# The high parts of q's, k's, gate's and value's weights begin 64 bytes further on in their tiles

## The chip, the cores and the metric

The kernel runs on one core of one Trainium2 chip. The metric is the device time of one execution in microseconds. Three runs of the kernel before took 966.67, 966.77 and 966.89 us; the median is 966.77 us.

## The reference

One layer of a bidirectional encoder for 256 tokens of width 2048, in float32:

```
h = rmsnorm(x, norm1_g);  q, k, v, u = split(h @ w_in)        # 1536, 512, 512, 512 columns
a = rmsnorm(window_attention(q, k, v, sink), attn_out_g)      # 12 heads of 128, 4 of k and v
f = rmsnorm(fourier_mix(u, w_fourier), fourier_out_g)         # 4 groups of 128
x = x + concat(a, f) @ w_out
h = rmsnorm(x, norm2_g);  gate, val = split(h @ w_up)         # 5504 columns each
x = x + (gelu(conv3(gate) + dw_b) * val) @ w_down
y = rmsnorm(x, normf_g)
```

The weights are 2048 x 2560 (`w_in`), 2048 x 2048 (`w_out`), 2048 x 11008 (`w_up`) and 5504 x 2048 (`w_down`). The work is matrix products.

## The kernel before

**Two parts for each operand.** Products run in the type float32r. To keep precision, each operand is split into a high part (a copy in float32r) and a low part (the operand less its high part). A product is then the sum of three: high by high, high by low, low by high.

**Units.** Weights come in units, tiles of 128 partitions x 2048 elements. `load` (L139) starts the DMA of a unit into one of three `raw` buffers, on SyncE's queue. `split` (L153) makes the high part on ScalarE (L160) and the low part on VectorE (L161); both go to tiles that `parts_of` (L145) takes, three buffers for `hi` and three for `lo`. The tiles are 2176 elements wide, 128 more than a unit has. `parts_of` returns 2048 of them, from element `s` on. For units 0 to 7 (u's four and v's four) `s` is `UV_SHIFT`, 16 elements or 64 bytes; for all others it is 0. The units in order: 0 to 3 u, 4 to 7 v, 8 to 23 q and k (16 heads), 24 to 39 the output projection, and then 86 of gate and value, 43 each, with the late rows of the down projection among them.

**Two ways to multiply.** `moving_weights` (L290) streams the weights, 512 columns at a time, past a part of the activations that is loaded into TensorE; three matmuls for each block of 128 rows (L296 to L298). It serves u, v, the output projection and the late rows of the down projection; `by_parts` (L1022 to L1024) and `last_product` (L1161 to L1163) do the same with other operands. `still_weights` (L302) loads a 128 x 128 block of the weights and streams the activations past it. It serves q, k, gate and value. The activations lie in the four tiles `hT` (after the second norm they are named hU), where each block of 128 rows has its 256 high and 256 low columns side by side. So one matmul over 512 columns does high by high and high by low (L307), and one over 256 columns low by high (L308):

```python
for k in kk:
    h = hT[k // 4][:, k % 4, :]
    s = slice(k * P, (k + 1) * P)
    nc.tensor.matmul(ps, hi[:, s], h, start=k == 0, stop=False)
    nc.tensor.matmul(ps[:, 0:S], lo[:, s], h[:, 0:S], start=False, stop=k == NK - 1)
```

A unit has 16 such pairs of matmuls. Each matmul has a load of its weights of its own, which the profile shows as PEld.

**Order.** The program is written out by hand; there is no scheduler. `unit` (L339) runs a unit's matmuls, then posts of earlier units, then the split of the unit two ahead; that split starts the load of the unit three further on. In the feed-forward part a list (`ff_items`, L68) gives the order: gate and value tiles of the first eight, then, for four groups, gate and value units that take turns with products of the down projection (`split_product` L908, seven products of two column halves, 56 in all), and at the end the late rows, the last three tiles' gate and value, and the last products. `ff_step` (L949) does there what `unit` does. The products' weights are split into the same `hi` and `lo` buffers, from element 0 on.

Of the kernel before, what the change touches and what calls it, by code (L numbers as in the profile page):

```python
# [30 lines left out]

U_HEAD, U_ROW = 16, 768

UV_SHIFT = 16

V_G2, V_GA, V_GF, V_DW, V_DB, V_SINK = 0, 16, 28, 32, 161, 204
V_N = 216
# [30 lines left out]
def ff_items():  # L68


    def ups(tiles):
        return [(kind, j) for j in tiles for kind in ("gate", "val")]

    items = ups(range(8))
    for g in range(N_GROUPS):
        todo = {
            "u": ups(range(8 * g + 8, 8 * g + 16)),
            "s": [("product", g, c, p) for c in range(2) for p in PRODUCTS[c]],
        }
        items += [todo[c].pop(0) for c in PATTERN]  # L80
        assert not any(todo.values())
    items += [("down", 0, c) for c in range(4)] + ups(LAST)
    items += [("down", 1, c) for c in range(4)] + [("last", c) for c in range(4)]
    return items
# [3 lines left out]
def block_kernel(  # L88
# [26 lines left out]
    def f32(ap):  # L115
        return ap.bitcast(F32)
# [4 lines left out]

    units = [(w_u_x[i], 2048) for i in range(4)] + [(w_in[i], 2048) for i in range(20)]
    units += [(w_out[i], 2048) for i in range(16)]
    n_front = len(units)
    items, up_index = ff_items(), {}
    for n, it in enumerate(items):
        if it[0] == "product":
            continue
        up_index[n] = len(units)
        if it[0] in ("gate", "val"):  # L130
            units.append((w_up[2 * it[1] + (it[0] == "val")], 2048))
        elif it[0] == "down":
            units.append((w_down_late[4 * it[1] + it[2]], 2048))
        else:
            units.append((w_down_last[it[1]], 512 * len(LAST)))
    RAW = 3
    raws, halves = {}, {}

    def load(i):  # L139
        if i < len(units) and i not in raws:  # L140
            src, n = units[i]
            raws[i] = wp.tile([P, 2048], F32, tag="raw", name=f"raw{i}", bufs=RAW)
            nc.sync.dma_start(raws[i][:, 0:n], src)

    def parts_of(i):  # L145
        s = UV_SHIFT if i < 8 else 0
        halves[i] = tuple(
            wp.tile([P, 2176], F32R, tag=h, name=f"{h}{i}", bufs=3)[:, s : s + 2048]
            for h in ("hi", "lo")
        )  # L150
        return halves[i]

    def split(i):  # L153

        if i >= len(units):
            return
        n = units[i][1]
        raw = raws[i]
        hi, lo = parts_of(i)
        nc.scalar.activation(hi[:, 0:n], raw[:, 0:n], AF.Copy)  # L160
        nc.vector.tensor_tensor(lo[:, 0:n], raw[:, 0:n], f32(hi[:, 0:n]), ALU.subtract)  # L161
        load(i + RAW)
        load_more(i + RAW)

# [29 lines left out]
    def u_part(k, o, n, m=1):  # L194

        rows = ux[k // 4][:, (k < 4) * U_HEAD :].rearrange("p (k c) -> p k c", k=4)
        return rows[:, k % 4 : k % 4 + m, o : o + n]
# [26 lines left out]
    def load_more(i):  # L224

        if i == 6:
            nc.sync.dma_start(chan, c_chan)
            nc.sync.dma_start(wfs, wf)
            nc.sync.dma_start(pos, c_pos)
        if i == 7:  # L230
            nc.sync.dma_start(vec[:, 0:V_N], vecs)
            nc.sync.dma_start(rel, c_rel)
# [118 lines left out]
    for k in range(NK):  # L351
        c, q = k // 4, k % 4
        if q == 0:
            hi, lo = (t.rearrange("p (k c) -> p k c", k=4) for t in parts_of(c))
        n = 1 if c < 2 else 2
        if k == 0:
            nc.vector.tensor_copy(hi[:, 0, :], u_part(0, 0, FW)[:, 0, :])
        split_scaled(hk(k), u_part(k, FW, S)[:, 0, :], g1[:, k : k + 1])
        if q % n == 0:
            w, h = u_part(k, 0, FW, n), hi[:, q : q + n, :]  # L360
            if k > 0:
                nc.scalar.activation(h, w, AF.Copy)
            nc.vector.tensor_tensor(lo[:, q : q + n, :], w, f32(h), ALU.subtract)
        if k < 4:

            for p, w in enumerate([hi, hi, lo]):
                for b in range(2):
                    o = p % 2 * S + b * P
                    nc.tensor.matmul(
                        ps_u[b], hk(k)[:, o : o + P], w[:, q, :],  # L370
                        start=k == 0 and p == 0, stop=False,
                    )
        else:
            for b in range(2):
                moving_weights(
                    *halves[c], 512, [k], hk, b, ps_u[b], False, k == NK - 1, q0=q
                )
        if q == 3:
            del halves[c]
# [387 lines left out]
    for n, (c, kq) in enumerate(OUT_ORDER):  # L767
        i = N_OUT + n
# [334 lines left out]
    for n, it in enumerate(items):  # L1103
# [26 lines left out]
        else:  # L1130
            kind, g, c = it
            hi, lo = halves.pop(up_index[n])
# [11 lines left out]
    i = up_index[n]  # L1144
# [147 lines left out]
```

## Time and profile before

| | |
|---|---|
| median of three runs | 966.77 us |
| profiled execution | 966.83 us |
| its span, first to last instruction | 965.1 us |
| mean granted TensorE clock | 0.998 |
| matmuls, weight loads | 5083, 5083 |
| L160, L161 (the splits) | 133 each; mean 1903 and 2276 ns |
| L307 for gate and for value | 688 each |
| L308 for gate and for value | 688 each |
| L307 for q and for k | 192 and 64 |
| DMA | 211.58 MB, 219 GB/s on the mean |

The profile is of one execution. PE is TensorE's matmuls, PEld its loads of weights, DVE VectorE, ACT ScalarE, POOL GpSimd. A row of the timeline gives the start and the duration of an instruction in microseconds, the engine, the line, what is written and read, and the shape. The duration of a matmul (0.39 us for 512 columns) holds its way through the array, and matmuls overlap; how fast they follow each other is seen from the starts. A row of the windows view gives a stretch, its length, and for each engine the busy time in it with the number of instructions in brackets.

### The profile page before, as it was taken

The numbers are of one execution on the slowest core, as the hardware profiler recorded it, in microseconds if no ns is written. First come the engines' busy times: TensorE is split into PE (matmuls) and PEld (weight loads), VectorE is DVE, ScalarE is ACT, GpSimd is POOL, SyncE is SP. The second block draws the span as 40 slices with busy tenths as digits, with TensorE's granted clock in tenths as the row PEclk, the third lists the DMA queues.
The fourth block names the chain that finished last, engine by engine and source line by source line (L and its number), as shares of the span: only waits on it lengthen the run. The fifth ranks groups of instructions, "written<-read, shape, count | busy, mean of one in ns | idle before, by whom it ended". The sixth has DMA issues, their size and how long they took to land.

```text
span 965.1 us, 12764 instructions
## 1 busy us (share of the span) xinstructions
PE 955.5 (99%) x5083; PEld 820.0 (85%) x5083; DVE 746.4 (77%) x926; ACT 535.7 (56%) x650; POOL 44.6 (5%) x59
## 2 busy tenths in 40 slices
PE   9999999999999999999999999999999999999996
PEld 7888898888888888888888888888888888888885
DVE  7658877666576679786898877988778979888675
ACT  7656766554454446555555555565555655553533
POOL 0000000000000000000000000000000000000003
PEclk9999999999999999999999999999999999999999
DMA  9844444446446675977777787776977686765532
GB/s 369 333 169 144 162 139 167 138 169 218 176 174 230 243 224 181 279 242 257 223 256 235 235 292 242 254 240 208 292 245 245 205 282 209 233 233 211 195 132 88
DMA packets 31676, 211.58 MB, mean 219 GB/s; under 512 B 3456, under 2 KB 3712, under 8 KB 7424
## 3 DMA queue, kind: packets, MB, share of 16 engines
q1 hardware_dynamic: 28016, 184.55, 51.4%
q0 software_dynamic: 3600, 26.22, 14.5%
q8 instruction: 40, 0.66, 0.3%
q14 instruction: 20, 0.16, 0.0%
HBM read 208.65 MB, written 2.10 MB: 218 GB/s over the span
## 4 chain that ended last, share of the span: by engine, by line
PE 96%; DMA 1%; DVE 1%; ACT 1%; issue 0%; SPq 0%; POOL 0%; ACTq 0%; POOLq 0%
PE ps_val L307 17%; PE ps_gate L307 17%; PE ps_val L308 8%; PE ps_gate L308 8%; PE ps_q L307 5%; PE ps_P L1022 3%; PE ps_P L1024 3%; PE ps_P L1023 3%; PE ps_q L308 2%; PE ps_a L298 2%; PE ps_a L296 2%; PE ps_a L297 2%; PE ps_N L1022 2%; PE ps_N L1024 2%; PE ps_N L1023 2%; PE ps_k L307 2%
## 5 line engine op out<-in xcount | busy, mean ns | idle before, releaser
L161 DVE TENSOR_TENSOR lo<-raw,hi 128x2048 fp32r<-128x2048 f32 (+1 forms) x133 | 302.8, 2276 | 54.8 <-ACT hi L160 54.8
L160 ACT ACTIVATE hi<-raw 128x2048 fp32r<-128x2048 f32 (+1 forms) x133 | 253.1, 1903 | 60.6 <-PE ps_l L297 25.1
L307 PE MATMUL ps_gate<-hU,hi 128*128 128x512 f32 x688 | 242.9, 394 | 0.0
L307 PE MATMUL ps_val<-hU,hi 128*128 128x512 f32 x688 | 242.8, 394 | 0.0
L308 PE MATMUL ps_val<-hU,lo 128*128 128x256 f32 x688 | 193.0, 281 | 0.0
L308 PE MATMUL ps_gate<-hU,lo 128*128 128x256 f32 x688 | 193.0, 281 | 0.0
L307 PEld LDWEIGHTS ps_gate<-hU,hi 128*128 128x128 f32 x688 | 129.4, 188 | 30.0
L307 PEld LDWEIGHTS ps_val<-hU,hi 128*128 128x128 f32 x688 | 129.3, 188 | 30.0
L308 PEld LDWEIGHTS ps_gate<-hU,lo 128*128 128x128 f32 x688 | 129.0, 187 | 1.1
L308 PEld LDWEIGHTS ps_val<-hU,lo 128*128 128x128 f32 x688 | 128.9, 187 | 1.1
L809 ACT ACTIVATE ft_g<-ps_gate 128x256 f32<-128x256 f32 x43 | 16.5, 384 | 127.5 <-PE ps_gate L308 127.5
L809 ACT ACTIVATE ft_v<-ps_val 128x256 f32<-128x256 f32 x43 | 16.5, 385 | 97.1 <-PE ps_val L308 97.0
L307 PE MATMUL ps_q<-hT,hi 128*128 128x512 f32 x192 | 68.5, 397 | 0.0
L308 PE MATMUL ps_q<-hT,lo 128*128 128x256 f32 x192 | 54.0, 281 | 0.0
L1022 PE MATMUL ps_P<-hi_P,op_P 128*128 128x512 f32 x128 | 50.2, 392 | 0.0
L1024 PE MATMUL ps_P<-lo_P,op_P 128*128 128x512 f32 x128 | 50.1, 391 | 0.0
L1023 PE MATMUL ps_P<-hi_P,op_P 128*128 128x512 f32 x128 | 49.7, 389 | 0.0
L919 DVE TENSOR_TENSOR lo_N<-sumw,hi_N 128x2048 fp32r<-128x2048 f32 x16 | 36.6, 2290 | 10.1 <-ACT hi_N L918 10.1
L307 PEld LDWEIGHTS ps_q<-hT,hi 128*128 128x128 f32 x192 | 36.1, 188 | 8.0
L811 DVE TENSOR_TENSOR fa_g<-ps_gate,ft_g 128x256 f32<-128x256 f32 x43 | 18.2, 423 | 29.3 <-ACT ft_g L809 29.3
L296 PE MATMUL ps_a<-hi,cat 128*128 128x512 f32 x96 | 37.8, 394 | 0.0
L1022 PE MATMUL ps_N<-hi_N,op_N 128*128 128x512 f32 x96 | 37.7, 393 | 0.0
(326 smaller groups left out, 1606.1 us busy)
## 6 DMA issues: line engine op xcount, KB each, us to landing
raw<-in_w_up SPq DMA_DIRECT2D x86, 1024.0 KB, 5.0
raw<-in_w_in SPq DMA_DIRECT2D x20, 1024.0 KB, 4.8
raw<-in_w_out SPq DMA_DIRECT2D x16, 1024.0 KB, 4.8
sumw<-in_w_down POOLq DMA_DIRECT2D x16, 1024.0 KB, 8.6
raw<-in_w_down_late SPq DMA_DIRECT2D x8, 1024.0 KB, 4.8
ux<-in_w_u_x SPq DMA_DIRECT2D x2, 1536.0 KB, 12.9
raw<-in_w_down_last SPq DMA_DIRECT2D x4, 768.0 KB, 4.2
xs<-in_x SPq DMA_DIRECT2D x4, 512.0 KB, 18.4
```

Source lines behind the costliest of these rows:

```text
L160: nc.scalar.activation(hi[:, 0:n], raw[:, 0:n], AF.Copy)
L161: nc.vector.tensor_tensor(lo[:, 0:n], raw[:, 0:n], f32(hi[:, 0:n]), ALU.subtract)
L296: nc.tensor.matmul(ps, ah, wh, start=first and q == q0, stop=False)
L297: nc.tensor.matmul(ps, al, wh, start=False, stop=False)
L298: nc.tensor.matmul(ps, ah, wl, start=False, stop=last and q == q0 + len(kk) - 1)
L307: nc.tensor.matmul(ps, hi[:, s], h, start=k == 0, stop=False)
L308: nc.tensor.matmul(ps[:, 0:S], lo[:, s], h[:, 0:S], start=False, stop=k == NK - 1)
L809: nc.scalar.activation(tmp, ps[:, S : 2 * S], AF.Copy)
L919: nc.vector.tensor_tensor(lo, src, f32(hi), ALU.subtract)
L1022: nc.tensor.matmul(ps, o[:, 0, p, :], hi[:, s], start=first and p == 0, stop=False)
L1023: nc.tensor.matmul(ps, o[:, 1, p, :], hi[:, s], start=False, stop=False)
L1024: nc.tensor.matmul(ps, o[:, 0, p, :], lo[:, s], start=False, stop=last and p == 3)
```

## The change

A list gives each unit two starts, one for its high and one for its low part. For u and v both stay at 16 elements. For q, k, gate and value the high part begins at 16 and the low part at 0. The output projection and the down projection stay at 0.

```diff
-UV_SHIFT = 16
+SHIFT = 16
...
     units += [(w_out[i], 2048) for i in range(16)]
+    shifts = [(SHIFT, SHIFT)] * 8 + [(SHIFT, 0)] * 16 + [(0, 0)] * 16
...
         if it[0] in ("gate", "val"):
             units.append((w_up[2 * it[1] + (it[0] == "val")], 2048))
+            shifts.append((SHIFT, 0))
+            continue
         elif it[0] == "down":
             units.append((w_down_late[4 * it[1] + it[2]], 2048))
         else:
             units.append((w_down_last[it[1]], 512 * len(LAST)))
+        shifts.append((0, 0))
...
     def parts_of(i):
-        s = UV_SHIFT if i < 8 else 0
         halves[i] = tuple(
             wp.tile([P, 2176], F32R, tag=h, name=f"{h}{i}", bufs=3)[:, s : s + 2048]
-            for h in ("hi", "lo")
+            for h, s in zip(("hi", "lo"), shifts[i])
         )
         return halves[i]
```

## The prediction

> **What bounds the kernel now.** I read the page's busy line and its chain first, then the view of who waits for whom on TensorE, and then, because that engine turns out to be full, start times of single matmuls in the timeline.
>
> ```profile
> span 965.1 us, 12764 instructions
> PE 955.5 (99%) x5083; PEld 820.0 (85%) x5083; DVE 746.4 (77%) x926; ACT 535.7 (56%) x650; POOL 44.6 (5%) x59
> ...
> PE 96%; DMA 1%; DVE 1%; ACT 1%; issue 0%; SPq 0%; POOL 0%; ACTq 0%; POOLq 0%
> ```
>
> ```profile
> PE ps_warm L243 <- POOL ones L235: 1.0, 1, 1.0
> PE ps_u L298 <- DVE lo L363: 0.5, 1, 0.5
> PE ps_l L296 <- DVE xs L1029: 0.2, 1, 0.2
> PE ps_u L369 <- ACT hT L250: 0.2, 1, 0.2
> ```
>
> TensorE (PE) is busy for 99% of the span and is 96% of the chain that ended last. All its waits for other engines sum to 1.9 us. So only one thing can move the end by more than a couple of microseconds: how far apart matmuls start. The split of the weights (L160, L161), the loads and the posts lie beside it.
>
> Most of that time is L307 and L308, `still_weights`: 16 times per unit, a matmul that streams 512 columns of h past the high part of the weights and one that streams 256 columns past the low part. I call these two a pair. 102 units (16 of q and k, 86 of gate and value) make 1632 pairs. While one matmul streams, the next one's weights are loaded (PEld): the low part's load lies beside the 512-column stream, the next high part's beside the 256-column one.
>
> How long does a pair take? The windows view on L307, with counts, and two timeline rows for q:
>
> ```profile
> core 0: us, PE busy (x) PEld busy (x), PEclk, DMA share, GB/s
> 283.98:368.78 84.80, 84.80 (x241) 44.98 (x240) 1.00 0.64 223
> 885.54:919.03 33.49, 33.49 (x96) 17.87 (x95) 1.00 0.52 187
> ```
>
> ```profile
> 158.44 0.39 PE L307 MATMUL ps_q<-hT,hi 128*128 128x512 f32 x1
> ...
> 164.08 0.40 PE L673 MATMUL ps_o<-pt,v_hi 128*128 128x256 f32 x2
> ```
>
> The first stretch runs from the first matmul of one gate unit to the end of another, with 15 units in it and no product between: 240 pairs (240 weight loads; one matmul of the 241 began before it) in 84.80 us, 353.3 ns each. The second is the last six units: 96 pairs in 33.49 us, 348.9 ns each. The q unit: 16 pairs in 5.64 us, 352.5 ns. The instructions, the addresses modulo 128 and the clock (PEclk 1.00) are the same, and still there are two rates, a slow one and a fast one. Start times show the slow one to be a cycle of three pairs:
>
> ```profile
> 295.29 0.40 PE L307 MATMUL ps_gate<-hU,hi 128*128 128x512 f32 x1
> 295.52 0.28 PE L308 MATMUL ps_gate<-hU,lo 128*128 128x256 f32 x1
> 295.64 0.39 PE L307 MATMUL ps_gate<-hU,hi 128*128 128x512 f32 x1
> 295.87 0.28 PE L308 MATMUL ps_gate<-hU,lo 128*128 128x256 f32 x1
> 295.99 0.40 PE L307 MATMUL ps_gate<-hU,hi 128*128 128x512 f32 x1
> 296.22 0.28 PE L308 MATMUL ps_gate<-hU,lo 128*128 128x256 f32 x1
> 296.35 0.40 PE L307 MATMUL ps_gate<-hU,hi 128*128 128x512 f32 x1
> ```
>
> Three pairs take 1.06 us (295.29 to 296.35). What would be the least? Streams of equal matmuls show it:
>
> ```profile
> 921.76:955.08 33.32, 33.32 (x148) 1.00 0.23 82
> ```
>
> ```profile
> 955.20 0.28 PE L1162 MATMUL ps_e<-hi,act 128*128 128x256 f32 x1
> ...
> 957.12 0.28 PE L1163 MATMUL ps_e<-lo,act 128*128 128x256 f32 x1
> ```
>
> The first stretch holds 147 matmuls of 512 columns (the 148th is the tail of an earlier one): 226.7 ns each. The second has 17 matmuls of 256 columns from the first row to the last, so 16 steps in 1.92 us, 120.0 ns each. A pair at these two is 346.7 ns, which I call the floor. The kernel pays 2.2 ns over it per pair in the fast cycle and 6.6 ns in the slow one. Rows that are rounded to 10 ns don't tell which of the two steps pays: in the cycle above the three long steps sum to 0.69 us (0.68 at the floor), the three short ones to 0.37 (0.36).
>
> **What the change does, part by part.** It moves no instruction: on all five engines the order and the waits are the same, and so are the allocations. The `hi` slice of the 102 units starts 64 bytes later. In the built program's allocation hT and hU lie at 96 modulo 128 bytes, every `hi` and `lo` tile at 32, and the operands of products, output projection and last tiles at 32. So in the two streams at the floor, and in v's (both parts already shifted to 96, hT at 96), what streams and what is loaded beside it have the same place modulo 128. In the pairs they are 64 apart, both for the high and the low part. After the change the high part's load has the same place as the h that streams; the low part's is still 64 apart.
>
> *Splits.* L160 writes, and L161 reads, a `hi` that begins 64 bytes on. v's units have that already; rows of DVE for one of them and for the first k unit, then of ACT for the same two:
>
> ```profile
> 44.02 2.29 DVE L161 TENSOR_TENSOR lo<-raw,hi 128x2048 fp32r<-128x2048 f32 x1
> 51.57 2.29 DVE L161 TENSOR_TENSOR lo<-raw,hi 128x2048 fp32r<-128x2048 f32 x1 [2.52 <-ACT hi L160]
> ```
>
> ```profile
> 38.84 1.91 ACT L160 ACTIVATE hi<-raw 128x2048 fp32r<-128x2048 f32 x1
> 49.63 1.91 ACT L160 ACTIVATE hi<-raw 128x2048 fp32r<-128x2048 f32 x1
> ```
>
> 2.29 and 2.29, 1.91 and 1.91 us: no cost. If there were one, TensorE would cover it, with DVE at 77% and ACT at 56%. The DMAs write `raw`, which stays.
>
> *Pairs.* The trace of before has no pair with the high part in the same place, so I bound it. One end is the floor, 346.7 ns, reached wherever places are the same. The other is the slow cycle, 353.3 ns, the worst that lasts. One load of the two comes to the favourable place, so I take half of what the fast cycle still pays: (346.7 + 348.9) / 2 = 347.8 ns for all pairs. The sum:
> - gate and value, slow: the 240 pairs above and, at the same rate, the 32 ahead of them: 272 x (353.3 - 347.8) = 1.5 us
> - the other 1104 pairs of gate and value: 1104 x (348.9 - 347.8) = 1.2 us
> - q and k: 256 pairs; all fast would give 0.3 us, all at 352.5 ns 1.2 us; I take 0.9 us
>
> Together 3.6 us.
>
> *Products.* They come between ups, one after each, with unshifted weights. A stretch of 13 ups and 13 products:
>
> ```profile
> 371.54:479.88 108.34, 73.23 (x209) 39.10 (x208) 1.00 0.77 239
> ```
>
> 208 pairs at 348.9 are 72.6 us, 156 product matmuls at 226.7 are 35.4 us; 0.4 us are left, 0.03 us for each change from pairs to products and back, 1.7 us for all 56. I count none of it as gained: the load beside the last 256 columns is then the product's operand, whose place stays. If pairs ran at the floor and so led into products without loss, it would be gained too.
>
> *Sum.* The profiled execution took 966.83 us, 1.73 us of it outside the span of 965.1; the median of the runs shown is 966.77, so they agree. 966.83 - 3.6 = 963.2 us.
>
> [...] The two floor streams show no sign of where a tile lies by itself: v's matmuls (33.20 to 33.65 for two) at 96 and the last tiles' at 32 both step by 0.23.
>
> ```profile
> 33.20 0.39 PE L297 MATMUL ps_v<-hi,hT 128*128 128x512 f32 x1
> ...
> 33.65 0.39 PE L296 MATMUL ps_v<-hi,hT 128*128 128x512 f32 x1
> ```
>
> [...]
>
> **The rivals.**
>
> *All the way to the floor* (part of my case, its far end): 272 x 6.6 + 1104 x 2.2 = 4.2 us, q and k 256 x up to 5.8 = 1.5, products 1.7: 7.4 us, 959.4 us. For it: every stream with the same places is at the floor. Against: the low part's load stays 64 apart, and it lies beside the long step, which seems to pay as much as the short one.
>
> *No effect.* Where the two reads do not meet at all, only the order and the mixture of 512 and 256 columns make the excess, and the place changes nothing: 966.8 us. For it: two rates exist with the same places, so something besides the place decides, and one of the two loads isn't moved. Against: nothing but the pairs is off the floor for long. [...] If the cycles are merely redrawn and all pairs fall into the fast one, it is 272 x 4.4 = 1.2 and about 0.7 for q and k: 964.9 us.
>
> *The slow cycle everywhere, slower than before.* The pairs lock into a three-pair cycle whose rate depends on how they are entered: the long gate and value stretch is slow from its entry until the first product at 368.78, and everything after is fast. A high part that moves by 64 bytes may shut the fast cycle off, because its load now asks for the same place as the 256-column stream, the shortest one, with the least time to hide a delay of the load. Its price is 353.3 - 348.9 = 4.4 ns on the 1104 pairs and about 64 of q and k that are fast: 5.1 us, 972.0 us. It decides from the point where three pairs after a product take 1.06 us and not 1.05. For it: the slow cycle is stable for 240 pairs once entered. Against: same places never show such a cycle.
>
> **How the numbers follow.** The pairs gain, between the fast cycle and the floor (959.4 to 964.9): 0.47, and the likeliest, at 963.2. No effect: 0.20, at 966.8. Slow cycle in most or all units: 0.33, up to 972.0. A measurement here tells about 0.2% from no change, 1.9 us, so the cases give faster 0.47, same 0.20, slower 0.33. The range takes the floor and the slow cycle with half a microsecond each for the stalls at q and k: 959.0 to 972.5. For my own case alone it is 959.4 to 964.9.
>
> **What the profile after would show.** My case: after the change the stretch from the second gate unit to the first product, 240 pairs, takes 83.2 to 83.7 us in place of 84.80, and the last 96 pairs about 33.4 or less in place of 33.49; splits stay at 1.91 and 2.29. No effect: both stretches as they are. Slow cycle: the last 96 pairs take 33.9 us, and an up with its product grows by 0.07 us. I am wrong in the mechanism if the pairs' rate changes while that of the three-pair cycle doesn't, if the streams of equal matmuls leave 226.7 ns, or if TensorE begins to wait for DVE or ACT.

## The result, and the profile after

The kernel after takes 965.63 us (median of 21 runs, 965.23 to 966.01); the kernel before, beside it, 966.94 us (21 runs, 966.44 to 967.70). The ratio is 0.9985, with a 95% interval of 0.9979 to 0.9991: 1.3 us or 0.15% faster, less than the 0.2% that the prediction set as its bound for a difference. The forecast was 963.2.

The page of the kernel after, its busy line and the shares of the chain that ended last:

```profile
span 963.6 us, 12764 instructions
...
PE 954.2 (99%) x5083; PEld 819.5 (85%) x5083; DVE 746.2 (77%) x926; ACT 535.7 (56%) x650; POOL 44.5 (5%) x59
...
PE 96%; DMA 1%; DVE 1%; ACT 1%; issue 0%; SPq 0%; POOL 0%; ACTq 0%; POOLq 0%
```

And all that TensorE waits for in it (in total, times, longest, us):

```profile
PE ps_warm L247 <- POOL ones L239: 1.0, 1, 1.0
PE ps_u L373 <- ACT hT L254: 0.2, 1, 0.2
PE ps_u L302 <- DVE lo L367: 0.2, 1, 0.2
PE ps_l L300 <- DVE xs L1033: 0.2, 1, 0.2
```

The number of instructions and the full TensorE are as in before, and the waits too, but for one that is 0.3 us shorter and lies ahead of the first k pair (lines of the file have moved on by four: L307 and L308 are L311 and L312 now). So the 1.3 us lie in how closely matmuls follow each other. The same three stretches of L311 as in the prediction, in the windows view of the kernel after:

```profile
283.04:367.04 84.00, 84.00 (x241) 45.01 (x240) 1.00 0.66 226
369.77:478.11 108.34, 73.42 (x209) 39.11 (x208) 1.00 0.76 239
883.94:917.54 33.60, 33.60 (x96) 17.86 (x95) 1.00 0.53 186
```

The 240 pairs ahead of the first product took 84.80 us and take 84.00: from 353.3 to 350.0 ns a pair. The last 96 took 33.49 and take 33.60: from 348.9 to 350.0, a little slower. The 13 ups with 13 products take 108.34 as before. There is one rate for gate and value now, where there were two. Its cycle in the timeline of the kernel after:

```profile
294.24 0.39 PE L311 MATMUL ps_gate<-hU,hi 128*128 128x512 f32 x1
294.48 0.27 PE L312 MATMUL ps_gate<-hU,lo 128*128 128x256 f32 x1
294.59 0.40 PE L311 MATMUL ps_gate<-hU,hi 128*128 128x512 f32 x1
294.82 0.28 PE L312 MATMUL ps_gate<-hU,lo 128*128 128x256 f32 x1
294.94 0.39 PE L311 MATMUL ps_gate<-hU,hi 128*128 128x512 f32 x1
```

Two pairs take 0.70 us (294.24 to 294.94), and then the pattern repeats. In before it was three pairs in 1.06 us.

Where the time went can be read from the starts of four matmuls. The first pair of k and the first pair of gate, in the timeline of the kernel after and then of the kernel before:

```profile
55.27 0.48 PE L311 MATMUL ps_k<-hT,hi 128*128 128x512 f32 x1
...
259.32 0.40 PE L311 MATMUL ps_gate<-hU,hi 128*128 128x512 f32 x1
```

```profile
55.41 0.48 PE L307 MATMUL ps_k<-hT,hi 128*128 128x512 f32 x1
...
260.14 0.40 PE L307 MATMUL ps_gate<-hU,hi 128*128 128x512 f32 x1
```

With the ends of the windows above, and those of the same windows of before in the prediction, this gives three stretches:

| stretch | before, us | after, us | gained, us |
|---|---|---|---|
| first k pair to first gate pair (q, k, attention, output projection) | 204.73 | 204.05 | 0.68 |
| first gate pair to first product | 108.64 | 107.72 | 0.92 |
| first product to the last six units | 516.76 | 516.90 | -0.14 |
| the last six units | 33.49 | 33.60 | -0.11 |

Together 1.35 us. The span is 1.5 us shorter because this execution also came to its first k pair 0.14 us earlier; that part of the program is not touched, and the medians differ by 1.31.

### The profile page after: what moved, and what is told of

It reads as the page before. It is cut to its first block, busy times and chain, and to the rows that moved or that the text cites. A ratio compares the mean times of both kernels' runs of the same rounds, so it can differ in the third digit from the quotient of the medians.

```text
span 963.6 us, 12764 instructions
## 1 busy us (share of the span) xinstructions
PE 954.2 (99%) x5083; PEld 819.5 (85%) x5083; DVE 746.2 (77%) x926; ACT 535.7 (56%) x650; POOL 44.5 (5%) x59
## 4 chain that ended last, share of the span: by engine, by line
PE 96%; DMA 1%; DVE 1%; ACT 1%; issue 0%; SPq 0%; POOL 0%; ACTq 0%; POOLq 0%
PE ps_gate L311 17%; PE ps_val L311 17%; PE ps_val L312 8%; PE ps_gate L312 8%; PE ps_q L311 5%; PE ps_P L1027 3%; PE ps_P L1028 3%; PE ps_P L1026 3%; PE ps_q L312 2%; PE ps_a L302 2%; PE ps_a L300 2%; PE ps_a L301 2%; PE ps_N L1027 2%; PE ps_N L1028 2%; PE ps_N L1026 2%; PE ps_k L311 2%
## 5 line engine op out<-in xcount | busy, mean ns | idle before, releaser
L311 PE MATMUL ps_val<-hU,hi 128*128 128x512 f32 x688 | 242.9, 396 | 0.0
L311 PE MATMUL ps_gate<-hU,hi 128*128 128x512 f32 x688 | 242.9, 396 | 0.0
L312 PE MATMUL ps_gate<-hU,lo 128*128 128x256 f32 x688 | 192.4, 280 | 0.0
L312 PE MATMUL ps_val<-hU,lo 128*128 128x256 f32 x688 | 192.4, 280 | 0.0
L311 PEld LDWEIGHTS ps_val<-hU,hi 128*128 128x128 f32 x688 | 129.4, 188 | 30.4
L311 PEld LDWEIGHTS ps_gate<-hU,hi 128*128 128x128 f32 x688 | 129.4, 188 | 30.4
L312 PEld LDWEIGHTS ps_gate<-hU,lo 128*128 128x128 f32 x688 | 130.0, 189 | 1.1
L312 PEld LDWEIGHTS ps_val<-hU,lo 128*128 128x128 f32 x688 | 130.0, 189 | 1.0
L311 PE MATMUL ps_q<-hT,hi 128*128 128x512 f32 x192 | 68.1, 398 | 0.0
L312 PE MATMUL ps_q<-hT,lo 128*128 128x256 f32 x192 | 53.6, 279 | 0.0
L311 PEld LDWEIGHTS ps_q<-hT,hi 128*128 128x128 f32 x192 | 36.1, 188 | 8.0
```

## The experiments

To compare kernels I write the place of a loaded block against the start of the activations that stream past it, in bytes, high part first. The places are those of the built program's allocation; the profile does not show them. The activations begin at 96 modulo 128 bytes and also modulo 256. Before is (-64, -64), after is (0, -64). "First rate" is that of the 240 pairs ahead of the first product, "last rate" that of the last 96 pairs.

The place theory was at first that each load's place by itself acts on the rate of the pairs, and in the end that the places of the two loads, taken together, do. Its rivals: that the distance between the high and the low part decides, one load's place against the other's (the distance theory, later called the step theory); that any move of a part out of a common place changes something, in the split or elsewhere, whatever the activations' place; and that what runs ahead of a pair picks its rate (the entry theory), at first with the place of no account. Each expectation tells what these give for its kernel. The kernels of a group ran on one chip beside runs of before.

| kernel | places | us | ratio to before, 95% interval | first rate, ns | last rate, ns |
|---|---|---|---|---|---|
| before | (-64, -64) | 966.9 to 967.1 | | 353.3 | 348.9 |
| after | (0, -64) | 965.63 | 0.9985 (0.9979 to 0.9991) | 350.0 | 350.0 |
| lo64 | (-64, 0) | 953.14 | 0.9856 (0.9840 to 0.9872) | 340.0 | 340.2 |
| both64 | (0, 0) | 964.50 | 0.9971 (0.9960 to 0.9982) | 346.7 | 346.7 |
| hi128 | (+64, -64) | 970.53 | 1.0034 (1.0021 to 1.0048) | 353.4 | 353.1 |
| h64 | mixed | 970.77 | 1.0036 (1.0023 to 1.0049) | 349.7 | 350.0 |
| hi256 | (+192, -64) | 967.24 | 1.0002 (0.9992 to 1.0011) | 353.3 | 349.0 |
| hi64_lo128 | (0, +64) | 963.19 | 0.9958 (0.9944 to 0.9973) | 346.7 | 346.9 |
| lo128 | (-64, +64) | 961.68 | 0.9943 (0.9928 to 0.9958) | 346.7 | 346.6 |
| h448 | (0, 0) | 969.20 | 1.0022 (1.0013 to 1.0032) | 346.7 | 353.2 |
| qk_only | q, k (0, -64) | 966.23 | 0.9992 (0.9983 to 1.0001) | 353.3 | 349.0 |
| prod64 | (-64, -64) | 970.85 | 1.0041 (1.0026 to 1.0055) | 353.3 | 349.0 |
| lo64_w64 | (-64, 0) | 954.40 | 0.9870 (0.9856 to 0.9885) | 340.0 | 350.0 |
| lo64_w192 | (-64, 0) | 967.17 | 1.0003 (0.9993 to 1.0012) | 340.0 | 340.1 |

### Which of the two parts

**lo64** moves the low parts and leaves the high ones.

```diff
-    shifts = [(SHIFT, SHIFT)] * 8 + [(SHIFT, 0)] * 16 + [(0, 0)] * 16
+    shifts = [(SHIFT, SHIFT)] * 8 + [(0, SHIFT)] * 16 + [(0, 0)] * 16
...
-            shifts.append((SHIFT, 0))
+            shifts.append((0, SHIFT))
```

> Only the low parts of q, k, gate and value begin 64 bytes on (high parts at 0). Place theory (a pair's rate is set by where each loaded block lies against the h that streams beside it, modulo 128 bytes, each load by itself): one of the two loads is in the same place as h, as in the changed kernel, but the one beside the 512-column stream; a third rate between 346.7 and 353.3 ns, not a cycle of three pairs at 353.3. Distance theory (what counts is that high and low part are 64 bytes apart from each other, so that successive loads alternate): the same as the changed kernel, 350.0 ns a pair in gate and value, 965.6 us. Entry theory (the address is irrelevant, each program redraws the cycle that it falls into): any of 346.7, 348.9, 350.0 and 353.3, with units of one kind of entry at several rates.

Measured: 953.14 us. The first and the last stretch of pairs in the windows view of lo64, and its pairs in the timeline:

```profile
281.86:363.46 81.60, 81.60 (x241) 45.00 (x240) 1.00 0.67 232
872.75:905.41 32.66, 32.66 (x96) 17.86 (x95) 1.00 0.55 192
```

```profile
294.10 0.39 PE L311 MATMUL ps_gate<-hU,hi 128*128 128x512 f32 x1
294.33 0.28 PE L312 MATMUL ps_gate<-hU,lo 128*128 128x256 f32 x1
294.44 0.39 PE L311 MATMUL ps_gate<-hU,hi 128*128 128x512 f32 x1
294.67 0.28 PE L312 MATMUL ps_gate<-hU,lo 128*128 128x256 f32 x1
294.78 0.39 PE L311 MATMUL ps_gate<-hU,hi 128*128 128x512 f32 x1
```

240 pairs in 81.60 us are 340.0 ns each, and every pair takes the same 0.34 us: no cycle over several pairs. This is below the 346.7 ns that the prediction called the floor, and none of the three theories had it. So the two parts are not alike: the low one's load, which lies beside the 512-column stream, is the one to move. The high one's load, beside the 256-column stream, does better 64 bytes off, as the next kernel shows (346.7 ns with it level, against 340.0).

**both64** moves both parts, so that all places are equal.

```diff
-            shifts.append((SHIFT, 0))
+            shifts.append((SHIFT, SHIFT))
```

(The same is done in the list for q and k.)

> High and low parts of q, k, gate and value both begin 64 bytes on, so all loads are in the same place as h modulo 128. Place theory: the floor, 346.7 ns for every pair, and products entered without loss; about 959.5 to 961 us. Distance theory: both parts have one place again, so it behaves as the kernel before: 353.3 and 348.9 ns, 966.9 us. Entry theory: no forecast, between 959 and 972 us.

Measured: 964.50 us. The first and the last stretch in its windows view:

```profile
284.28:367.48 83.20, 83.20 (x241) 44.99 (x240) 1.00 0.67 228
883.39:916.67 33.28, 33.28 (x96) 17.85 (x95) 1.00 0.54 188
```

Equal places give 346.7 ns, just what the streams of equal matmuls sum to, though not step by step: on the mean over these 240 pairs, by the trace's starts in nanoseconds, the 512-column step is 231.8 ns and the 256-column step 114.8, where the equal streams have 226.7 and 120.0. The 959.5 to 961 us that the place theory gave are missed, because products were not entered without loss: between products a unit takes 5.55 us in place of 5.59, but the product after it 2.77 in place of 2.75. The gains of the two parts do not add: the low part at 0 is worth 13.3 ns over the first rate of before with the high part at -64 (353.3 to 340.0), and 3.3 with the high part at 0 (350.0 to 346.7).

### Is it a place, and with what period

**hi128** moves the high part by 128 bytes in place of 64.

```diff
-            shifts.append((SHIFT, 0))
+            shifts.append((2 * SHIFT, 0))
```

(And for q and k.)

> High parts begin 128 bytes on in place of 64, low parts at 0. If the place modulo 128 bytes is what counts (place and distance theory alike), this is the kernel before: gate and value from the second unit to the first product at 353.3 ns a pair, the last six units at 348.9, 966.9 us. If any shift does it (entry theory, or a split that gets cheaper), it differs from before, towards 965.6 us.

Measured: 970.53 us, slower than before. The first and the last stretch in its windows view:

```profile
284.29:369.10 84.81, 84.81 (x241) 45.42 (x240) 1.00 0.65 223
888.54:922.44 33.90, 33.90 (x96) 18.02 (x95) 1.00 0.53 187
```

A slow rate, 353 ns, holds in both stretches. If places counted modulo 128, as the prediction took them, this kernel would be before (a high part 64 ahead is 64 behind). It isn't, by 3.4 us. **hi256** moves the high part by 256 bytes.

```diff
-            shifts.append((SHIFT, 0))
+            shifts.append((4 * SHIFT, 0))
```

> High parts begin 256 bytes on, low parts at 0. Both theories now count places modulo 256 bytes, since 128 bytes were not the same as 0. Period of 256 bytes: the kernel before again, 353.3 ns a pair in gate and value up to the first product and 348.9 in the last six units, 967 us. Longer period: other rates, as 64 and 128 bytes had.

Measured: 967.24 us. The windows view of hi256:

```profile
283.71:368.51 84.80, 84.80 (x241) 44.98 (x240) 1.00 0.66 223
885.25:918.75 33.50, 33.50 (x96) 17.87 (x95) 1.00 0.53 187
```

84.80 and 33.50 us against 84.80 and 33.49 of before: both rates, the slow one and the fast one, are back. So a move by 256 bytes is none (+192 and -64 are the same place), and a move in itself costs or brings nothing. Places count modulo 256 bytes here: of the high part's two moves, 128 bytes take the last rate from 348.9 to 353.1 ns and 256 leave it at 349.0.

### Place against the activations, or of the parts to each other

**h64** was to move the activations in place of the weights, so that each load is 64 bytes further back.

```diff
-            wp.tile([P, 2176], F32R, tag=h, name=f"{h}{i}", bufs=3)[:, s : s + 2048]
+            wp.tile([P, 2080], F32R, tag=h, name=f"{h}{i}", bufs=3)[:, s : s + 2048]
...
-        t = base.tile([P, 4, 512], F32R, tag=f"hT{c}", name=f"hT{c}")
+        t = base.tile([P, 2080], F32R, tag=f"hT{c}", name=f"hT{c}")[:, 16:2064].rearrange("p (k c) -> p k c", k=4)
```

(No part of any weights is moved, hU's tiles and those of the products' weights are changed in the same way.)

> No weights are shifted (u and v neither); hT and hU begin 64 bytes on, so that h and all weights lie at 32 modulo 128. The hi and lo tiles are 96 elements narrower, a multiple of 128 bytes. Place theory: only the difference counts, so the same as with both parts shifted: 346.7 ns a pair and about 959.5 to 961 us. If the absolute place of the weights counts: as the kernel before, 966.9 us. Distance theory: as before too.

Measured: 970.77 us, and nothing follows from it. A tile of 2080 elements is 8320 bytes, which is no multiple of 256, so the three buffers and the four activation tiles lie at several places, and pairs meet loads at 0 or at -128 in turn:

```profile
285.68:369.61 83.93, 83.93 (x241) 45.04 (x240) 1.00 0.66 226
```

349.7 ns is the mean over pairs at these places. The streams of equal matmuls left their 226.7 ns as well (231.5 by their starts; the nine steps from 939.78 to 941.88 us in the timeline are 233.3 each); their operands lie in the same buffers. **h448** does it rightly: the activations are moved by 448 bytes in tiles of 2176 elements (8704 bytes, 34 x 256), the weights' tiles are 2048 wide and unshifted, and all places are equal, as in both64.

```diff
-        t = base.tile([P, 4, 512], F32R, tag=f"hT{c}", name=f"hT{c}")
+        t = base.tile([P, 2176], F32R, tag=f"hT{c}", name=f"hT{c}")[:, 112:2160].rearrange("p (k c) -> p k c", k=4)
```

> No weights are shifted, u and v neither; hT and hU begin 448 bytes on, which modulo 512 is 64 bytes back, and all other tiles keep their places modulo 512 (the hi and lo tiles are 512 bytes narrower). High and low parts then lie to h as they do with both shifted by 64 bytes, modulo 256. If only the relative place counts: as there, 346.7 ns a pair in gate and value, about 964.5 us. If the weights' own place counts: as the kernel before, 353.3 and 348.9 ns, 967 us.

Measured: 969.20 us, 4.7 us more than both64. The windows view of h448:

```profile
284.24:367.44 83.20, 83.20 (x241) 44.89 (x240) 1.00 0.66 228
887.58:921.49 33.91, 33.91 (x96) 17.85 (x95) 1.00 0.52 184
```

The first stretch is that of both64 to the last digit, 346.7 ns. After the products the pairs run at 353.2 ns in place of 346.7. So moving the activations does what moving the weights does, as long as a rate lasts. The splits of the first stretch write to the same places as in before, so where they write does not set the rate. But equal places allow more than one rate, and the place by itself does not tell which one comes. The two kernels differ in one more thing: in both64 the pairs' loads lie 64 bytes off the streams of the products ahead, in h448 level with them. This was not tried by itself.

**hi64_lo128** and **lo128** hold the distance between the parts apart from their places: in the one the low part lies 64 ahead of the high one, as in lo64, but at (0, +64); in the other 128 ahead, at (-64, +64).

```diff
-            shifts.append((SHIFT, 0))
+            shifts.append((SHIFT, 2 * SHIFT))
```

> High parts begin 64, low parts 128 bytes on. Step theory (what counts is how far the low part's place lies ahead of the high part's; 64 bytes ahead is best): as with the low part alone 64 bytes on, 340.0 ns a pair, about 953 us. Place theory (each load against the h that streams beside it, modulo 256): neither load lies where it lay there (high 64 behind h, low level with h), now high level, low 64 ahead, so another rate; the high part 64 bytes ahead of h cost most so far (353.3 ns), so 350 ns or more, 965 to 971 us.

```diff
-            shifts.append((SHIFT, 0))
+            shifts.append((0, 2 * SHIFT))
```

> Low parts begin 128 bytes on, high parts at 0. Step theory: the parts are 128 bytes apart, as with the high part 128 bytes on, modulo 256 the same distance: 353.3 ns a pair, about 970.5 us. Place theory: the high part lies 64 behind h as in the kernel before and in the best one, the low part 64 ahead of h: a rate of its own between 340 and 353.3 ns, and it differs from that of the high part at 128.

Measured: 963.19 and 961.68 us. The first stretch of hi64_lo128, and then that of lo128, in their windows views:

```profile
283.67:366.87 83.20, 83.20 (x241) 44.94 (x240) 1.00 0.66 228
```

```profile
283.50:366.70 83.20, 83.20 (x241) 45.01 (x240) 1.00 0.67 228
```

Both at 346.7 ns. If the distance of the parts decided, the first would be at lo64's 340.0 and the second at 353.3, as hi128 is, whose parts are 128 apart as well. Both miss by 6.7 ns: the step theory falls. (The place theory's own guess for the first, 350 ns or more, missed as well.) That one place effect for each load is summed up falls too, by the rates that the first stretch has. A low part at +64 gives 346.7 whether the high part is at -64 or at 0, while a low part at 0 gives 340.0 with the one and 346.7 with the other.

### What picks the rate

**qk_only** moves the high parts of q and k alone.

```diff
     shifts = [(SHIFT, SHIFT)] * 8 + [(SHIFT, 0)] * 16 + [(0, 0)] * 16
...
-            shifts.append((SHIFT, 0))
+            shifts.append((0, 0))
```

> The change for q and k alone; gate's and value's high parts stay at 0. The rate of a pair is set by the places in its own unit: the first gate pair starts about 0.8 us earlier than in the kernel before, as it did in the changed kernel, and gate and value keep 353.3 ns up to the first product and 348.9 in the last six units; about 966.3 us. Rival, that the phase is carried from stage to stage: gate and value then fall into other rates.

Measured: 966.23 us, which is not told from no change. The first k pair and the first gate pair of qk_only in the timeline:

```profile
56.09 0.48 PE L311 MATMUL ps_k<-hT,hi 128*128 128x512 f32 x1
...
260.13 0.40 PE L311 MATMUL ps_gate<-hU,hi 128*128 128x512 f32 x1
```

204.04 us lie between, as in after (204.05) and 0.69 less than in before; the rest is as before, with 353.3 and 349.0 ns. So the gain of q and k in after is their own, and gate and value take nothing over from it.

**prod64** leaves the pairs as in before and moves the products' weights, which TensorE streams, by 64 bytes.

```diff
-            shifts.append((SHIFT, 0))
+            shifts.append((0, 0))
...
-            wp.tile([P, 2176], F32R, tag=h, name=f"{h}_{p}_{g}{c}", bufs=3)[:, 0:2048]
+            wp.tile([P, 2176], F32R, tag=h, name=f"{h}_{p}_{g}{c}", bufs=3)[:, 16:2064]
```

(And (0, 0) for q and k.)

> Places of all pairs as in the kernel before; only the products' weights, which stream past their operands, begin 64 bytes on. Entry theory (the places give a pair a few lasting cycles, and what runs ahead of it picks one): 353.3 ns a pair up to the first product as before; after it the pairs are entered from products in another phase, so the units that alternate with products may leave 348.9 for 353.3 ns, an up unit then takes 5.65 us in place of 5.59. If the places alone fix the cycle: 5.59 us still. In both, the products are no longer at 226.7 ns a matmul if equal places make that rate; 672 matmuls, a few ns each, 967 to 972 us.

Measured: 970.85 us. The windows view of prod64, ahead of the products, 13 ups with 13 products, and the last six units:

```profile
284.02:368.82 84.80, 84.80 (x241) 44.98 (x240) 1.00 0.65 223
371.57:480.73 109.16, 73.91 (x208) 39.09 (x208) 1.00 0.77 237
889.56:923.06 33.50, 33.50 (x96) 17.87 (x95) 1.00 0.53 186
```

The pairs' instructions and places are those of before. Ahead of the products and in the last six units, which follow unmoved weights, they run as in before. Between products an up with its product takes 8.40 us (109.16 / 13) in place of 8.33. By starts and on the mean, a unit there takes 5.643 us in place of 5.588, which is a slow cycle, 352.7 ns a pair, and the product after it takes 2.755 in place of 2.745: most of the loss lies in pairs that were not touched. So with one and the same place both rates last, and the matmuls just ahead pick one of them.

The trace of before shows the same. Its first 12 gate pairs follow the output projection; then eight small matmuls (L749) cut in, and the pairs go on. The windows view of before on L307, for pairs ahead of the small matmuls and for pairs behind them:

```profile
260.49:263.63 3.14, 3.14 (x10) 1.69 (x10) 1.00 0.72 292
266.60:271.90 5.30, 5.30 (x16) 2.82 (x16) 1.00 0.36 150
```

Nine steps in 3.14 us are 348.9 ns each, 15 in 5.30 us are 353.3. So before was fast behind streams of 512 columns, and slow from the small matmuls to the first product.

**lo64_w64** and **lo64_w192** take lo64 and move what the other streams read, the weights of the output projection and of the down projection, by 64 and by 192 bytes.

```diff
-    shifts = [(SHIFT, SHIFT)] * 8 + [(SHIFT, 0)] * 16 + [(0, 0)] * 16
+    shifts = [(SHIFT, SHIFT)] * 8 + [(0, 16)] * 16 + [(16, 16)] * 16
...
-        shifts.append((0, 0))
+        shifts.append((16, 16))
...
-            wp.tile([P, 2176], F32R, tag=h, name=f"{h}_{p}_{g}{c}", bufs=3)[:, 0:2048]
+            wp.tile([P, 2176], F32R, tag=h, name=f"{h}_{p}_{g}{c}", bufs=3)[:, 16:2064]
```

(48 in place of 16 in the second, and (0, 16) for gate and value in both.)

> The best version so far (low parts of q, k, gate and value 64 bytes on, 953.1 us), and all weights that stream (output projection, late rows, products) 64 bytes on, so that what is loaded beside them lies 64 bytes behind. A load 64 behind let the 256-column matmuls of the best version run at 113.3 ns in place of 120.0. If it does the same for equal matmuls of 512 columns: 220 ns in place of 226.7, about 1,100 of them, some 7 us, 946 us. If equal places are the best for them: 230 ns or more, 956 us or more.

> As the run before, with the weights that stream 192 bytes on, so that what is loaded lies 64 bytes ahead of the stream modulo 256. If equal places are the best for equal matmuls of 512 columns: over 226.7 ns, 956 us or more. If any place off the stream's own is better: 220 ns, 946 us. The pairs stay at 340.0 ns up to the first product in either case.

Measured: 954.40 and 967.17 us; lo64 was 953.14. The first shows the last 147 matmuls of 512 columns in lo64_w64, the second those in lo64_w192, in the windows view of TensorE:

```profile
909.81:943.49 33.68, 33.68 (x149) 1.00 0.24 82
```

```profile
921.21:955.47 34.26, 34.26 (x148) 1.00 0.24 81
```

By the starts at their ends 147 steps lie in each: 229.1 and 233.1 ns, against 226.7 with equal places. So equal matmuls also step by their places: of the three tried the best is where the load and the stream agree, 2.4 ns more are taken with the load 64 bytes behind the stream, 6.4 with it 64 ahead (192 behind). The 220 ns that were hoped for came in neither. And the pairs after them change without being touched. The first stretch and one further on, in the windows views of lo64_w64 and of lo64_w192:

```profile
283.58:365.19 81.61, 81.61 (x241) 44.95 (x240) 1.00 0.68 232
873.47:907.07 33.60, 33.60 (x96) 17.86 (x95) 1.00 0.52 186
```

```profile
284.04:365.64 81.60, 81.60 (x241) 44.94 (x240) 1.00 0.68 232
368.43:477.45 109.02, 73.35 (x208) 39.10 (x208) 1.00 0.76 239
```

340.0 ns ahead of the first product in both. The last 96 pairs of lo64_w64 run at 350.0; between products, a unit of lo64_w192 takes 5.60 us, 350 ns a pair, though its last six units run at 340.1 again. So the rate goes by both, the place and what runs ahead: what the good place of the pairs brings can be lost through the places of what is multiplied ahead of them. Of all that was tried, lo64 is the best: 14.0 us less than before on the same chip (967.11), where after is 1.3 less, and it differs from after only in which of the two parts is moved.

## Why the prediction was right or wrong

**The time.** 965.63 us lies within the stated 959.0 to 972.5, but that says little, since the range spans the floor and the slow cycle. It lies outside the 959.4 to 964.9 of the prediction's own case, and by its bound of 0.2% the outcome is the one called same, to which it gave 0.20.

**What bounds it, and what the change can reach: right.** TensorE stays full (99% busy), its waits sum to 1.6 us, and all that changed is the distance of matmuls.

**Splits: right.** In after, for a v unit (both parts moved) and the first k unit (the high part moved), the timeline of VectorE shows 2.29 us, as in before:

```profile
44.17 2.29 DVE L165 TENSOR_TENSOR lo<-raw,hi 128x2048 fp32r<-128x2048 f32 x1
...
51.44 2.29 DVE L165 TENSOR_TENSOR lo<-raw,hi 128x2048 fp32r<-128x2048 f32 x1 [2.52 <-ACT hi L164]
```

**Pairs: right that the place sets the rate, wrong in how.** This is the step that failed: "One load of the two comes to the favourable place, so I take half of what the fast cycle still pays: (346.7 + 348.9) / 2 = 347.8 ns for all pairs." It measured 350.0, so the fast pairs even lost. Four things in it were not so:
- Half of the way is no bound. The two ends were taken from pairs with both loads off and from streams with both loads equal, and a mixed place does not lie between them: 350.0 at (0, -64), above the fast cycle, and 340.0 at (-64, 0), below the floor. The sum of two equal streams (226.7 + 120.0) is what pairs with equal places cost in both64, and no least value.
- The favourable place was given to the wrong load. The low part's load decides most: 353.3 to 340.0 ns with it moved (lo64), to 350.0 with the high one moved (after).
- The two steps of a pair were taken to pay alike ("seems to pay as much as the short one"), as far as rounded rows told. The trace's starts, in nanoseconds and averaged over the 240 slow pairs of before, give 233.7 for the long step and 119.7 for the short one, against 226.7 and 120.0 in equal streams: all of the excess lay in the long step, beside the low part's load. In after they are 233.2 and 116.8, in lo64 226.7 and 113.3. The load that was moved lay beside the step that paid nothing; what after gained came from that step all the same, which fell below the 120.0 of the floor.
- Places were counted modulo 128. Against this argument hi128 stands (970.53 us, 3.4 above before), and for 256 hi256 (967.24 us, 0.2 above); (0, -64) would have been the same in both, so this error cost nothing here.

By terms (four units, 64 pairs, lie ahead of the 240, not 32, and the stretch begins with the third gate unit; this moves the sum by less than 0.2 us): the slow pairs were to gain 1.5 us and gained 0.92 with what surrounds them (353.3 to 350.0 on 240 pairs is 0.80); the 1104 fast ones were to gain 1.2 us and gave up 0.25 with the products among them; q and k were to gain 0.9 and gained 0.68. That is 1.35 in place of 3.6 us.

**Products: not as counted.** I took no gain at the change from pairs to products. By starts and at the median, a unit between products takes 5.599 us in place of 5.587, and the product after it 2.734 in place of 2.746: the pairs' loss of 12 ns comes back at the product, and the 13 together stay at 108.34 us. Nobody had forecast this. Without it the ups between products would have cost 56 x 0.012 = 0.7 us, half of the whole gain.

**What the profile was to show.** 240 pairs in 83.2 to 83.7 us: 84.00, missed. The last 96 in 33.4 or less: 33.60, missed. Of the signs of a wrong mechanism none came: the three-pair cycle went with the rate, TensorE waits for nothing new, and streams of equal matmuls stay at 226.7 ns; the same last 147 matmuls in the windows view of TensorE in after:

```profile
920.27:953.59 33.32, 33.32 (x148) 1.00 0.24 82
```

**The rivals.** *No effect* falls as a mechanism, with both rates moved (353.3 and 348.9 ns to 350.0) and an interval that leaves out 1, though the time is nearer to it (966.8) than to the forecast. It had the place change nothing; the same instructions in the same order take 340.0 (lo64) to 353.4 ns (hi128) a pair in the first stretch, by the places of the two operands. Its relative, cycles that are only redrawn (964.9), came nearest in time: the slow cycle and the fast one did become one, but at a rate of its own. *The slow cycle everywhere* did not come here; at (+64, -64) it did, at 970.5 us where 972.0 had been its price. That a cycle depends on how it is entered, on which this rival stood, is shown by prod64 (a unit between products takes 5.643 us in place of 5.588). *All the way to the floor* needs both parts (both64), and then takes 964.5 us and not 959.4: q and k gain only 0.06 us between the first k pair and the first gate pair (204.67 us by their starts), and the products take more and not less.

**What stays open.** What in the chip makes the rate go by the places of loads and streams is not shown. Nor is it shown by what a pair's cycle remembers the matmuls ahead of it, or whether 340.0 ns is the least: places 128 bytes off come only mixed with others (h64), and further pairs of places were not tried.

## What to carry to other kernels

Where TensorE is full, write down the place of each loaded block against the operand that streams past it, modulo 256 bytes (here a move of 128 cost 3.4 us and one of 256 changed 0.2), keep the strides of tiles multiples of 256 (tiles of 8320 bytes left h64 at several places and a mean of 349.7 ns), and try the places of each operand one by one: here moving the high parts was worth 0.15% and moving the low parts 1.4%. Read the rate from starts over many matmuls and look for a cycle over several of them; a stretch that changes its rate without a change of its own points to what runs ahead of it (prod64, 5.588 to 5.643 us a unit). Don't take a rate measured on equal matmuls as the least for mixed ones (346.7 ns by the sum of equal streams, 340.0 in lo64), and don't halve a gain because half of the operands were moved (347.8 ns by halving, 350.0 measured).

## What the runs showed of the hardware that had not been expected

- Matmul steps depend on places, modulo 256 bytes where that was tried (last rate 348.9 ns in before, 353.1 in hi128, 349.0 in hi256): a pair of 512 and 256 columns takes 340.0 (lo64), 346.7 (both64), 350.0 (after) or 353.3 ns (before), and a 512-column matmul in a stream of equal ones 226.7 (after), 229.1 (lo64_w64) or 233.1 (lo64_w192).
- One place can have two lasting rates: 348.9 and 353.3 ns at (-64, -64) (before), 346.7 and 353.2 at (0, 0) (h448), 340.0 and 350.0 at (-64, 0) (lo64_w64). What is multiplied ahead picks one (in prod64 349.0 behind unmoved weights and 352.7 between the moved ones), and it held for as long as pairs followed each other (in before 240 pairs, 84.80 us).
- The four steady first rates, 340.0, 346.7, 350.0 and 353.3 ns, are 102, 104, 105 and 106 times 3.333 ns, and 226.7 is 68 times. This is worked out from these rows alone; 348.9, 229.1 and 233.1 ns are no whole counts of it, so that rates come in such steps is not shown.
